# Where a scan's input copies stand among attention steps, in a hybrid block on one core

## The chip, the cores and the metric

The kernel runs on one core of a Trainium2 chip. The time is what the device takes for one execution, in microseconds (us); the median of several runs is given. Besides these runs one execution was taken by the profiler, and all rows below come from it.

The core has five engines that matter here, each with its own queue of instructions, done strictly in order: TensorE (PE in the rows; its weight loads are PEld), VectorE (DVE), ScalarE (ACT), GpSimd (POOL) and SyncE (SP), which issues the loads. An instruction waits on semaphores for what it needs from other engines, and all that stands behind it in its queue waits too.

## The reference, cut to what matters

One layer of a decoder on 512 positions of width 1024, in float32: a normalisation, an input projection, three token mixers on its parts, gates, an output projection and a residual, then a gated convolutional feed-forward part of inner width 2816 with its own normalisation and residual, and a last normalisation. Two of the three mixers are touched here:

```
proj = h @ w_in                                   # qa, ka, va, qd, kd, vd, u, g
ya   = banded_attention(qa, ka, va, 127, sinks)   # A: 8 heads, 4 blocks of 128 positions
x_t  = Abar * x_(t-1) + Bbar u_t                  # C: diagonal complex state space,
y    = Re(C x) + D u                              #    32 groups of 16 channels, 64 states each
out  = x + (gates * (ya, yb, yc) @ w_branch) @ w_out
```

B is a dilated attention that comes later in the kernel.

## The kernel before

Every large product is done in three TensorE passes: each operand is split into a high part and a low part of a rounded format (`whi`, `wlo` for weights), and high times high, high times low and low times high are summed in one PSUM bank (`mm3`, `mm3m`). ScalarE makes the high part of a weight (a copy, L66), VectorE the low one (a subtraction, L92); for some weights GpSimd does every second low part.

The work is a list of **units**, mostly one output tile of 128 x 512 each: 24 matmuls of 128 x 512. Unit 0 finishes the projection of `u`; units 1 to 4 are the queries of mixer A, 5 and 6 its keys and values (`kA`, `vA`), 7 to 14 its gates, 15 to 24 the projections of mixer B, 25 to 68 branch products, more gates and the gated unit of mixer C, 69 to 76 the output projection (`out_unit`), and then come the feed-forward units. Two units share one chunk of weights, loaded by SyncE into one of two `raw` buffers and split in two pieces.

The order within each engine's queue is the order in which the program emits the instructions. `run` walks the units. At unit `u` it emits first the splits that are due for the next chunk, then the steps that `before(u, ...)` has listed for this unit, and then the unit's matmuls and what uses their result:

```
fs = plan.get(u, []) + later
...
if u in AUX_FIRST:          # (7, 11, 15, 19, 33, 35)
    for f in fs: f()
    fs = []
...                          # splits of the next chunk, those listed in early
for f in fs: f()
fn()
```

In the units named in `AUX_FIRST` the listed steps come ahead of the splits. `early` lists (chunk, pieces) that are split in a given unit; a piece can only be split when one of four piece buffers is free, and a chunk that is due in the next unit is split in this one in any case. A chunk whose pieces are all split has the load of a later one issued.

The steps that are interleaved with units 3 to 24:

- `attn_a(i)`, one for each block of 128 queries, gives control back after each step. Step 1: score matmuls of four heads into two PSUM banks `sc` (L802), and masks with row maxima on VectorE (L809), which free these banks. Step 2: the same for the other four heads, then the exponentials on ScalarE (L818) and the scaling on VectorE (L308). Step 3: transposes (L832) and their copies. Step 4: products with the values (L838); for blocks 1 to 3 a second round of these, and `ya` at the end.
- `ssm_bd(j)`, `ssm_inj(j)`, `ssm_ob(j)`, `ssm_e(j)` prepare slice `j` of four of mixer C. `ssm_bd` ends with the four copies (VectorE, L663) that lay `u` out by position within groups of four as `US[j]`. `ssm_inj` transposes the input matrices into two `pt` banks and copies them out as `INJ[j]` (ScalarE), and fills `TZ[j]`. `ssm_cpow` computes the powers `Vw` on GpSimd, with temporaries `vt`. `ssm_e` computes tables `E` on GpSimd.
- `ssm_m1(j)`: first step, 16 small matmuls of `INJ[j]` with `US[j]` into two `sc` banks (L723), four products with `E`, and two scans on VectorE; second step, four products on VectorE and two on GpSimd that give the states `X`. `ssm_m2(j)`: 48 small matmuls of `US[j]` with `TZ[j]` and of `X` with `OB[j]`, copied out as `yS`.
- `to_nat` transposes the values of mixer A into a `pt` bank, unit 8.

Nearly all temporaries (`US`, `INJ`, `E`, `vt`, score tiles, `th`, and the results of projections) come from one pool `s` of 46 buffers. A request takes a buffer when the program emits it, and its first writer waits until the last user of the buffer's former content is done.

In `out_unit` the first call has SyncE load `x` again for the residual; the last matmul of a token tile is followed by the residual add on VectorE and a sum of squares on ScalarE. `ko[0]` to `ko[3]` are the four chunks of `w_out`, used in units 69 to 72 in this order, the last two again in 73 and 74.

Of the kernel before, what the change touches and what calls it, by code (L numbers as in the profile page):

```python
# [31 lines left out]
def hybrid_block(  # L32
# [19 lines left out]
    def slot(shape, dt=F32, name="s"):  # L52
        return sl.tile(shape, dt, tag="s", name=name)
# [4 lines left out]
    def bank(tag, shape=(128, 512), name=None):  # L58
        return psp.tile(list(shape), F32, tag=tag, bufs=PSB[tag], name=name or tag)
# [4 lines left out]
    def copy_act(o, i, scale=None):  # L64
        if scale is None:
            S.activation(o, i, AF.Copy)  # L66
        else:
            S.activation(o, i, AF.Copy, scale=scale)
# [165 lines left out]
    def before(u, *fns):  # L234
        plan.setdefault(u, []).extend(fns)
# [81 lines left out]
    def tt(o, a, b, op, eng=None):  # L317
        emit(lambda: (eng or V).tensor_tensor(o, a, b, op=op))  # L318
        return o
# [332 lines left out]
    def expand(dst, src, j, scale=None):  # L652

        for g in range(2):
            p = slice(64 * g, 64 * g + 64)
            copy_act(dst[p, :, :, g, :], src[p].rearrange("p k (t j) h -> p t k j h", j=4)[:, :, :, j, :], scale=scale)

    def ssm_bd(j):
        for i in range(2):
            expand(BDs[j % 2][i], W[0][:, i], j)  # L660
        US[j] = slot([128, 4, 128], name="us")
        for tau in range(4):
            V.tensor_copy(US[j][32 * tau:32 * tau + 32],  # L663
                          uT[0][32 * j:32 * j + 32].rearrange("p t (c a) -> p t c a", a=4)[:, :, :, tau])

    def ssm_inj(j):
        bd = BDs[j % 2]
        INJ[j] = [slot([128, 4, 128], name="inj") for _ in range(2)]
        for i in range(2):
            pb = bank("pt")  # L670
            for t in range(4):
                PE.transpose(pb[:, t * 128:(t + 1) * 128],
                             bd[i][:, t].rearrange("p k g h -> p (k g h)"), ident)
            copy_act(INJ[j][i][:, :, :], pb[:, :].rearrange("p (t c) -> p t c", t=4))
        pk = bank("o", (128, 4, 32))
        for t in range(4):
            for i in range(2):
                PE.matmul(pk[:, t, :], bd[i][:, t].rearrange("p k g h -> p (k g h)"),
                          V0b[i][:, 4 * t + j].rearrange("p g h -> p (g h)"), start=(i == 0), stop=(i == 1))
        tz = TZ[j]  # L680
        for ti in range(4):
            for to in range(ti + 1, 4):
                b = 3 - (to - ti)
                copy_act(tz[32 * ti:32 * ti + 32, :, to, :], pk[32 * b:32 * b + 32, :, :])
        for ti in range(4):
            tt(tz[32 * ti:32 * ti + 32, :, ti, :], pk[96:128, :, :],
               DI[0][96:128].rearrange("p (t j) c -> p t j c", j=4)[:, :, j, :], ADD)

    def ssm_ob(j):
        for i in range(2):  # L690
            expand(OB[j][i], Vw[0][:, i], j, None if i == 0 else -1.0)
# [5 lines left out]
    def ssm_e(j):  # L697
        def v(tab):
            return tab.rearrange("p (t j) b -> p t j b", j=4)[:, :, j, :]

        b = [v(t)[:, :, None, :].to_broadcast([128, 4, 8, 16]) for t in eb]
        a = [v(t)[:, :, :, None].to_broadcast([128, 4, 8, 16]) for t in ea]
        E = [slot([128, 4, 8, 16], name="E") for _ in range(2)]
        t0 = slot([128, 4, 8, 16], name="et")
        tt(E[0], b[0], a[0], MUL, G)
        tt(t0, b[1], a[1], MUL, G)
        tt(E[0], E[0], t0, SUB, G)
        tt(E[1], b[0], a[1], MUL, G)
        tt(t0, b[1], a[0], MUL, G)
        tt(E[1], E[1], t0, ADD, G)  # L710
        Es[j] = [e[:, :, :, :].rearrange("p t a b -> p (t a b)") for e in E]
        A4s[j] = slot([128, 4, 128], name="a4")
        V.tensor_copy(A4s[j], mag4.rearrange("p (t j) -> p t j", j=4)[:, :, j:j + 1].to_broadcast([128, 4, 128]))
        V.memset(A4s[j][:, :, 0:1], 0.0)

    def ssm_m1(j):
        Er, Ei = Es.pop(j)
        s = []
        inj = INJ.pop(j)
        for i in range(2):  # L720
            pb = bank("sc", (128, 4, 128))
            for t in range(4):
                PE.matmul(pb[:, t, :], inj[i][:, t, :], US[j][:, t, :], start=True, stop=True)  # L723
            s.append(pb[:, :, :].rearrange("p t c -> p (t c)"))
        a, b, zr, zi = (slot([128, 512], name="z")[:, :] for _ in range(4))
        tt(zr, s[0], Er, MUL)
        tt(a, s[1], Ei, MUL)
        tt(zi, s[1], Er, MUL)
        tt(b, s[0], Ei, MUL)
        tt(zr, zr, a, ADD, G)  # L730
        tt(zi, zi, b, SUB, G)
        a4 = A4s.pop(j)[:, :, :].rearrange("p t c -> p (t c)")
        V.tensor_tensor_scan(a, a4, zr, 0.0, op0=MUL, op1=ADD)
        V.tensor_tensor_scan(b, a4, zi, 0.0, op0=MUL, op1=ADD)
        yield
        X = [slot([128, 4, 128], name="X") for _ in range(2)]
        x3 = slot([128, 512], name="xt")[:, :]

        def sh(v):
            return v.rearrange("p (t c) -> p t c", c=128)[:, :, 0:127]  # L740

        for i in range(2):
            G.memset(X[i][:, :, 0:1], 0.0)
        tt(zr, a, Er, MUL)
        tt(x3, b, Ei, MUL)
        tt(X[0][:, :, 1:128], sh(zr), sh(x3), SUB, G)
        tt(zi, a, Ei, MUL)
        tt(b, b, Er, MUL)
        tt(X[1][:, :, 1:128], sh(zi), sh(b), ADD, G)
        Xs[j] = X  # L750
        yield

    def ssm_m2(j):
        if not yS:
            yS.append(y8([128, 4, T], name="yS"))
        X, tz, us, ob = Xs.pop(j), TZ.pop(j), US.pop(j), OB.pop(j)
        py = bank("o", (128, 4, 128))
        for t in range(4):
            PE.matmul(py[:, t, :], tz[:, t].rearrange("p a b -> p (a b)"), us[:, t, :], start=True, stop=False)
            for i in range(2):  # L760
                PE.matmul(py[:, t, :], ob[i][:, t].rearrange("p k g h -> p (k g h)"), X[i][:, t, :],
                          start=False, stop=(i == 1))
        for tau in range(4):
            o = yS[0][32 * j:32 * j + 32].rearrange("p t (c a) -> p t c a", a=4)[:, :, :, tau]
            copy_act(o, py[32 * tau:32 * tau + 32])


    def to_nat(src, name, strided=False):

        pb = bank("pt")  # L770
        v = src[:, :].rearrange("p (i r) -> p r i", r=4) if strided else src[:, :].rearrange("p (b i) -> p b i", b=4)
        for b in range(4):
            PE.transpose(pb[:, b * 128:(b + 1) * 128], v[:, b, :], ident)
        o = slot([128, 4, 128], name=name)
        copy_act(o, pb[:, :].rearrange("p (b c) -> p b c", b=4))
        return o

    proj = {}
# [10 lines left out]
    VA = []  # L789
# [677 lines left out]
        for ci in range(2):  # L1467
            add(ko[2 * half + ci], out_unit(ko[2 * half + ci], pair, half, ci, last))
    for u, i, n in ((63, 0, 1), (64, 0, 2), (65, 0, 3), (66, 0, 4), (66, 1, 1), (67, 1, 2), (68, 1, 3), (69, 1, 4),
                    (69, 2, 1), (70, 2, 2), (71, 3, 1), (72, 3, 2)):  # L1470
        early.setdefault(u, []).append((ko[i], n))
    u_up = len(units)
    for c in range(NF // 2):
# [52 lines left out]
    def st_(g):  # L1526
        return lambda: next(g)

    CP = ssm_cpow()
    A = [attn_a(i) for i in range(4)]  # L1530
    B = [attn_b(i) for i in range(2)]
    M = [ssm_m1(j) for j in range(4)]
    before(0, lambda: pump(99), ssm_b, lambda: pump(6), ssm_phase)
    before(1, lambda: pump(9))
    before(2, lambda: pump(9))
    before(3, lambda: ssm_bd(0))
    before(4, lambda: ssm_inj(0), lambda: ssm_bd(1), lambda: ssm_e(0), st_(CP))
    before(5, lambda: ssm_inj(1), lambda: ssm_bd(2))
    before(6, lambda: ssm_inj(2), lambda: ssm_bd(3), st_(CP), st_(A[0]))
    before(7, st_(A[0]), lambda: ssm_inj(3))  # L1540
    before(8, lambda: VA.append(to_nat(proj["vA"], "VA")), lambda: ssm_ob(0), lambda: ssm_ob(1))
    before(9, st_(A[0]), st_(M[0]), lambda: ssm_ob(2))
    before(10, lambda: ssm_ob(3), st_(A[0]), st_(M[0]), st_(A[1]))
    before(11, st_(A[1]))
    before(12, lambda: ssm_m2(0), lambda: ssm_e(1))
    before(13, st_(A[1]), st_(M[1]))
    before(14, st_(A[1]), st_(M[1]), st_(A[2]))
    before(15, st_(A[1]), st_(A[2]))
    before(16, lambda: ssm_m2(1), lambda: ssm_e(2))
    before(17, st_(A[2]), st_(M[2]))  # L1550
    before(18, st_(A[2]), st_(M[2]), st_(A[3]))
    before(19, st_(A[2]), st_(A[3]))
    before(20, lambda: ssm_m2(2), lambda: VB.setdefault(0, [to_nat(proj["vB", 0], "VB0")]), lambda: ssm_e(3))
    before(21, st_(A[3]), st_(M[3]), lambda: VB[0].append(to_nat(proj["vB", 0], "VB1", True)))
# [51 lines left out]
```

## Time and profile before

| | |
|---|---|
| median of 3 runs | 820.75 us (820.46 to 821.0) |
| the profiled execution | 820.41 us, of which 818.6 us are its span |
| TensorE busy | 796.6 us, 97% of the span |
| VectorE busy | 540.5 us, 66% |
| ScalarE busy | 392.8 us, 48% |
| GpSimd busy | 165.3 us, 20% |
| TensorE's granted clock, mean | 0.994 of full speed |

The span is the time from the first to the last instruction of the core; 1.8 us of the execution lie outside it. Busy times are sums over instructions. The matmuls are pipelined and their ends are modelled, so a TensorE that is busy throughout may still issue at a lower rate; the starts of its instructions tell more than its busy time.

### The profile page before, as it was taken

Reading aid. Unit: us, or ns where it says so; the run is one execution under the profiler, and the core shown is the slowest. Engines: PE = TensorE matmul, PEld = TensorE weight load, DVE = VectorE, ACT = ScalarE, POOL = GpSimd, SP = SyncE. Lnnn points to the kernel's source line nnn. Section 1 sums busy time; section 2 is a strip of 40 time slices with the busy share of each in tenths; the row PEclk is TensorE's granted clock in tenths of the full one; section 3 lists DMA queues with packets and bytes.
Section 4 is the critical chain, followed back from the end, with each engine's and each line's share of the span. In section 5 each row is a group of like instructions: output and inputs, shape, how many; then the busy total and the mean of one; then the engine's idle time right before and its main releaser. Section 6 shows DMA issues by size and latency. Waiting matters only on the chain.

```text
span 818.6 us, 10655 instructions
## 1 busy us (share of the span) xinstructions
PE 796.6 (97%) x4007; PEld 660.5 (81%) x4007; DVE 540.5 (66%) x1021; ACT 392.8 (48%) x725; POOL 165.3 (20%) x222
## 2 busy tenths in 40 slices
PE   8999799999999999999999999999999999999995
PEld 7978678788787888788887998888888888888884
DVE  7998676674636637363665456667666666888976
ACT  6446456456354555351434334444444444455553
POOL 6189723513200100014440000000000000011201
PEclk9999999999999999999999999999999999999998
DMA  8332031121322113122243253222333334589952
GB/s 245 104 104 82 21 103 53 52 73 53 81 95 66 54 52 104 63 92 102 104 187 121 64 186 111 99 79 83 101 103 102 104 104 128 207 241 347 294 157 102
DMA packets 76871, 94.70 MB, mean 116 GB/s; under 512 B 8944, under 2 KB 56340, under 8 KB 76820
## 3 DMA queue, kind: packets, MB, share of 16 engines
q1 hardware_dynamic: 73828, 88.74, 32.8%
q0 software_dynamic: 2992, 5.29, 3.8%
q8 instruction: 31, 0.51, 0.3%
q14 instruction: 20, 0.16, 0.1%
HBM read 89.80 MB, written 4.22 MB: 115 GB/s over the span
## 4 chain that ended last, share of the span: by engine, by line
PE 80%; POOL 8%; DVE 6%; ACT 2%; issue 2%; DMA 1%; POOLq 0%; SPq 0%; DVEq 0%; ACTq 0%
PE up L208 10%; PE up L209 10%; PE up L210 10%; PE mm L208 9%; PE mm L210 9%; PE mm L209 9%; PE p L214 4%; PE p L216 4%; PE p L215 4%; POOL esc L318 1%; POOL vt L318 1%; POOL t L318 1%; PE acc L215 1%; PE acc L216 1%; PE acc L214 1%
## 5 line engine op out<-in xcount | busy, mean ns | idle before, releaser
L92 DVE TENSOR_TENSOR wlo<-raw,whi 128x1024 fp32r<-128x1024 f32 (+1 forms) x104 | 123.0, 1192 | 94.5 <-ACT whi L66 94.4
L208 PE MATMUL up<-hTh,whi 128*128 128x512 f32 (+1 forms) x384 | 142.9, 372 | 0.0
L210 PE MATMUL up<-hTh,wlo 128*128 128x512 f32 (+1 forms) x384 | 142.8, 372 | 0.0
L209 PE MATMUL up<-hTl,whi 128*128 128x512 f32 (+1 forms) x384 | 142.8, 372 | 0.0
L66 ACT ACTIVATE whi<-raw 128x1024 fp32r<-128x1024 f32 (+1 forms) x126 | 126.1, 1013 | 18.3 <-PE p L216 10.6
L208 PE MATMUL mm<-hTh,whi 128*128 128x512 f32 (+1 forms) x336 | 133.1, 396 | 0.0
L210 PE MATMUL mm<-hTh,wlo 128*128 128x512 f32 (+1 forms) x336 | 130.1, 387 | 0.0
L209 PE MATMUL mm<-hTl,whi 128*128 128x512 f32 (+1 forms) x336 | 130.0, 387 | 0.0
L314 DVE SCALAR_TENSOR_TENSOR cc<-up,cpar,cc 128x511 f32<-128x511 f32 x88 | 65.9, 749 | 70.0 <-ACT cc L1146 68.4
L210 PEld LDWEIGHTS up<-hTh,wlo 128*128 128x128 f32 x384 | 72.4, 188 | 12.5
L208 PEld LDWEIGHTS up<-hTh,whi 128*128 128x128 f32 x384 | 72.4, 188 | 12.5
L209 PEld LDWEIGHTS up<-hTl,whi 128*128 128x128 f32 x384 | 72.4, 189 | 12.3
L208 PEld LDWEIGHTS mm<-hTh,whi 128*128 128x128 f32 x336 | 63.6, 189 | 14.5 <-issue 2.5
L1146 ACT ACTIVATE cc<-up,cpar 128x512 f32<-128x512 f32 x44 | 34.1, 775 | 85.2 <-PE up L210 85.2
L210 PEld LDWEIGHTS mm<-hTh,wlo 128*128 128x128 f32 x336 | 63.5, 189 | 13.0
L209 PEld LDWEIGHTS mm<-hTl,whi 128*128 128x128 f32 x336 | 63.7, 190 | 11.7
L185 POOL DMA_DIRECT2D raw<-in_w_down_dram x5 | 5.7, 1147 | 271.3 <-DVE wlo L92 221.1
L214 PE MATMUL p<-whi,op 128*128 128x512 f32 x146 | 56.9, 389 | 0.0
L216 PE MATMUL p<-whi,op 128*128 128x512 f32 x146 | 56.9, 389 | 0.0
L215 PE MATMUL p<-wlo,op 128*128 128x512 f32 x146 | 56.9, 389 | 0.0
L1028 ACT ACTIVATE th<-mm 128x512 f32<-128x512 f32 x24 | 14.3, 595 | 65.5 <-PE mm L210 65.4
L318 POOL TENSOR_TENSOR th<-th 128x512 f32<-128x512 f32 x15 | 23.8, 1607 | 69.9 <-DVE th L314 69.9
(314 smaller groups left out, 1386.9 us busy)
## 6 DMA issues: line engine op xcount, KB each, us to landing
raw<-in_w_up_dram SPq DMA_DIRECT2D x22, 1024.0 KB, 5.1
raw<-in_w_in_dram SPq DMA_DIRECT2D x18, 1024.0 KB, 5.1
raw<-in_w_down_dram SPq DMA_DIRECT2D x19, 512.0 KB, 8.1
big<-in_w_down_dram SPq DMA_DIRECT2D x16, 512.0 KB, 6.5
x<-in_x_dram SPq DMA_DIRECT2D x8, 512.0 KB, 6.9
raw<-in_w_in_dram SPq DMA_DIRECT2D x8, 512.0 KB, 5.2
raw<-in_w_out_dram SPq DMA_DIRECT2D x4, 1024.0 KB, 5.1
big<-in_w_down_dram POOLq DMA_DIRECT2D x5, 512.0 KB, 9.0
```

Source lines behind the costliest of these rows:

```text
L66: S.activation(o, i, AF.Copy)
L92: (lo_eng or V).tensor_tensor(view(lo), r, view(hi).bitcast(F32), op=ALU.subtract)
L208: PE.matmul(ps, wh, xh, start=first, stop=False)
L209: PE.matmul(ps, wh, xl, start=False, stop=False)
L210: PE.matmul(ps, wl, xh, start=False, stop=last)
L214: PE.matmul(ps, xh, wh, start=first, stop=False)
L215: PE.matmul(ps, xh, wl, start=False, stop=False)
L216: PE.matmul(ps, xl, wh, start=False, stop=last)
L314: emit(lambda: V.scalar_tensor_tensor(o, a, s, b, op0=op0, op1=op1))
L318: emit(lambda: (eng or V).tensor_tensor(o, a, b, op=op))
L1028: S.activation(t, ps, AF.Tanh, scale=0.5)
L1146: S.activation(dst, ps, AF.Identity, bias=cpar[:, 3, f:f + 1], scale=cpar[:, 2, f:f + 1])
```

## The change

The copies into `US[j]` become a function of their own, `ssm_us(j)`, and are called in units 7, 8, 10 and 11 and not in units 3 to 6, behind the attention step of their unit. In units 10, 14 and 18 the first step of the next attention block and the second step of the scan change places. The last chunk of output weights, `ko[3]`, is split in unit 70; it was listed for 71 and 72, of which 71 did both pieces.

```diff
     def ssm_bd(j):
         for i in range(2):
             expand(BDs[j % 2][i], W[0][:, i], j)
+
+    def ssm_us(j):
         US[j] = slot([128, 4, 128], name="us")
         for tau in range(4):
             V.tensor_copy(US[j][32 * tau:32 * tau + 32],
...
     for u, i, n in ((63, 0, 1), (64, 0, 2), (65, 0, 3), (66, 0, 4), (66, 1, 1), (67, 1, 2), (68, 1, 3), (69, 1, 4),
-                    (69, 2, 1), (70, 2, 2), (71, 3, 1), (72, 3, 2)):
+                    (69, 2, 1), (70, 2, 2), (70, 3, 2)):
         early.setdefault(u, []).append((ko[i], n))
...
-    before(7, st_(A[0]), lambda: ssm_inj(3))
-    before(8, lambda: VA.append(to_nat(proj["vA"], "VA")), lambda: ssm_ob(0), lambda: ssm_ob(1))
+    before(7, st_(A[0]), lambda: ssm_inj(3), lambda: ssm_us(0))
+    before(8, lambda: VA.append(to_nat(proj["vA"], "VA")), lambda: ssm_ob(0), lambda: ssm_ob(1), lambda: ssm_us(1))
     before(9, st_(A[0]), st_(M[0]), lambda: ssm_ob(2))
-    before(10, lambda: ssm_ob(3), st_(A[0]), st_(M[0]), st_(A[1]))
-    before(11, st_(A[1]))
+    before(10, lambda: ssm_ob(3), st_(A[0]), st_(A[1]), st_(M[0]), lambda: ssm_us(2))
+    before(11, st_(A[1]), lambda: ssm_us(3))
     before(12, lambda: ssm_m2(0), lambda: ssm_e(1))
     before(13, st_(A[1]), st_(M[1]))
-    before(14, st_(A[1]), st_(M[1]), st_(A[2]))
+    before(14, st_(A[1]), st_(A[2]), st_(M[1]))
     before(15, st_(A[1]), st_(A[2]))
     before(16, lambda: ssm_m2(1), lambda: ssm_e(2))
     before(17, st_(A[2]), st_(M[2]))
-    before(18, st_(A[2]), st_(M[2]), st_(A[3]))
+    before(18, st_(A[2]), st_(A[3]), st_(M[2]))
     before(19, st_(A[2]), st_(A[3]))
```

## Rows read from the trace of the kernel before

**Rows 1.** The page, busy time, share of the span and instructions of each engine.
```profile
PE 796.6 (97%) x4007; PEld 660.5 (81%) x4007; DVE 540.5 (66%) x1021; ACT 392.8 (48%) x725; POOL 165.3 (20%) x222
```

**Rows 2.** Waits of TensorE: who for whom, us in total, times, longest.
```profile
PE sc L802 <- DVE mxA L809: 3.1, 2, 2.0
PE pt L773 <- ACT inj L66: 3.0, 1, 3.0
...
PE acc L215 <- DVE wlo L92: 0.8, 1, 0.8
```

**Rows 3.** Stretches: length, then busy us of each engine, TensorE's clock, DMA.
```profile
86.00:109.00 23.00, 20.04 (x108) 16.96 (x108) 12.03 (x27) 15.27 (x42) 11.32 (x19) 0.93 0.14 46
98.30:101.70 3.40, 3.40 (x10) 2.62 (x9) 1.95 (x5) 3.31 (x8) 0.00 (x0) 0.51 0.00 0
138.00:430.00 292.00, 291.75 (x1495) 234.98 (x1494) 164.01 (x370) 135.44 (x285) 64.70 (x57) 1.00 0.27 86
```

**Rows 4.** Timeline of TensorE: start, us, instruction, [idle before and what ended it].
```profile
76.52 0.72 PE L802 MATMUL sc<-pj 64*128 64x128 f32 x8
...
82.32 0.39 PE L209 MATMUL mm<-hTl,whi 128*128 128x512 f32 x1
82.55 0.39 PE L210 MATMUL mm<-hTh,wlo 128*128 128x512 f32 x1
84.95 1.13 PE L802 MATMUL sc<-pj 64*128 64x128 f32 x8 [2.02 <-DVE mxA L809]
...
97.33 0.66 PE L773 MATMUL pt<-ident,pj 128*128 128x128 f32 x4 [2.96 <-ACT inj L66]
...
105.79 1.95 PE L723 MATMUL sc<-us,inj 128*128 128x128 f32 x16
...
122.12 1.81 PE L802 MATMUL sc<-pj 64*128 64x256 f32 x8 [1.14 <-DVE mxA L809]
...
140.15 0.48 PE L208 MATMUL mm<-hTh,whi 128*128 128x512 f32 x1
...
432.64 0.51 PE L215 MATMUL acc<-wlo,mh 128*128 128x512 f32 x1 [0.75 <-DVE wlo L92]
```

**Rows 5.** The chain that ended last, in order of time: start, us, what.
```profile
155.62 1.06 PE sc L802 x8
```

**Rows 6.** Timeline of VectorE, units 5 and 6.
```profile
70.25 1.22 DVE L318 TENSOR_TENSOR tz<-o,DI 32x128 f32<-32x128 f32 x4 [1.42 <-ACT tz L66]
71.48 5.22 DVE L663 COPY us<-uT 32x512 f32<-32x512 f32 x4
...
79.97 4.41 DVE L663 COPY us<-uT 32x512 f32<-32x512 f32 x4
```

**Rows 7.** The line of the copies: ns least, median, most; first and last start.
```profile
L663 DVE COPY us<-uT x16: 623/797/1624, 57.6 to 83.4; 32x512 f32<-32x512 f32 x16
```

**Rows 8.** Timelines of ScalarE and of GpSimd, end of unit 7.
```profile
96.68 1.28 ACT L66 ACTIVATE inj<-pt 128x512 f32<-128x512 f32 x2 [5.37 <-POOL Vw L318]
...
95.92 1.40 POOL L318 TENSOR_TENSOR Vw<-vt 128x256 f32<-128x256 f32 x2
```

**Rows 9.** Timeline of VectorE, units 7 to 12.
```profile
91.98 4.75 DVE L308 TENSOR_SCALAR smA<-smA,lA 128x128 f32<-128x128 f32 x8
...
117.19 0.69 DVE L318 TENSOR_TENSOR ya<-o,ya 128x512 fp32r<-128x512 f32 x1 [0.85 <-ACT ya L66]
...
121.30 0.41 DVE L809 CUSTOM_DVE_ANT_0 smA<-sc,maskA 128x256 f32<-128x256 f32 x1
...
125.06 1.08 DVE L314 SCALAR_TENSOR_TENSOR nmA<-mxA,nsink 128x8 f32<-128x8 f32 x1
...
133.91 1.22 DVE L92 TENSOR_TENSOR wlo<-raw,whi 128x1024 fp32r<-128x1024 f32 x1
```

**Rows 10.** Timelines of ScalarE and of VectorE, units 71 and 72.
```profile
430.28 1.99 ACT L66 ACTIVATE whi<-raw 128x1024 fp32r<-128x1024 f32 x2
...
427.64 0.69 DVE L318 TENSOR_TENSOR x<-x,acc 128x512 f32<-128x512 f32 x1 [4.19 <-DMA x<-in_x_dram]
```

## The prediction

> **What bounds the kernel now.** I began with the page. TensorE counts as busy for 796.6 us of a span of 818.6 us [rows 1], so no change of order among the other engines can win more than the waits of TensorE, plus what its clock loses behind them. The list of waits on TensorE alone is the second view: three of its entries lie at places that the diff touches, 3.1 us behind the mask of the attention scores, 3.0 us behind a copy of `inj`, 0.8 us behind the split of an output weight [rows 2]. The table of stretches is the third: from 138 to 430 us TensorE idles 0.25 us in 292, at full clock [rows 3], so whatever is won earlier is carried to the end and little is won there. In the same table the granted clock is 0.51 from 98.3 to 101.7 us, right behind the longest wait.
>
> TensorE's timeline gives the price of each wait. Matmuls of 0.39 us are issued 0.23 us apart (82.32, 82.55), so a wait shown as idle time costs 0.16 us more than the row says [rows 4].
>
> **The copies `US`, and the wait at 85 us.** `US[3]` stands at the end of unit 6 on VectorE, 79.97 to 84.38 us [rows 6], ahead of the masks of block 0's first scores. TensorE needs the banks that these masks free: it idles 2.02 us until 84.95, and the eight score matmuls then take 1.13 us where the eight of unit 6 took 0.72 [rows 4]. Without the copy the masks run from about 80.0, done well before 82.8. Gain 2.02 + 0.16 + (1.13 - 0.72) = 2.59 us.
>
> **The wait at 97 us.** The transposes of `vA` wait 2.96 us [rows 4] for the two copies of `inj` of slice 3, and ScalarE does these at 96.68 because it waited 5.37 us for GpSimd's last step of `Vw` (95.92) [rows 8]. The reference has no such dependence; it is a buffer's. The pool `s` hands out its 46 buffers and then always the one free longest. Counting requests in program order, `inj` of slice 3 is the 56th and 57th, and the eleven buffers free by then are, oldest first, `craw` (2), `braw` (2), `esc`, `wt` (2), `et`, `V0`, `vt` (2): it gets the two `vt`, which GpSimd writes until the end of `Vw`. With the four `US` requested behind it, it is the 52nd and 53rd and gets the two `wt`, whose last use is far back. The copies then follow block 0's exponentials at once, before TensorE is through unit 7. Gain 2.96 + 0.16 = 3.12 us. The clock: 0.51 over 3.40 us [rows 3] is 3.40 x 0.49 = 1.67 us, lost right behind an idle stretch of 3 us and, I take it, gone with it.
>
> The pair `vt` goes to `VA` and `US[1]` instead. On ScalarE `VA` then may wait for `Vw`, but behind it stand the copies into `OB`, which need `Vw` anyway, and the product with `VA` comes a whole unit later: nothing.
>
> **Where `US[0]` and `US[1]` go.** They land in units 7 and 8, where VectorE is busy for only 12.03 of 23 us [rows 3]; that idle time covers them. The tight point is `US[0]`: block 0's scaling ends at 91.98 + 4.75 = 96.73 [rows 9], 2.59 us earlier after the change, 94.1; 1.2 us of `TZ` adds follow [rows 6], then four copies at 0.62 us, the least of the sixteen, to 97.8, or 4.41 us in all, to 99.7 [rows 6, 7]. TensorE's scan matmuls of slice 0 need them at 105.79 - 7.4 = 98.4 [rows 4]. Upper bound 1.4 us, lower bound none; I take none, since without the copies in units 3 to 6 GpSimd's tables are through sooner and these copies then run beside an idle GpSimd.
>
> **Units 10 to 13.** Now the masks of block 1's first scores go ahead of the scan's second half. Before, TensorE waited 1.14 us at 122.12 for them, and the scores took 1.81 us where later ones take 1.06 [rows 4, 5]: gain 1.14 + 0.16 + 0.75 = 2.05 us. But VectorE must now do `US[2]` ahead of the second masks, and `US[3]` ahead of the low split of unit 13's weights (unit 11 is in `AUX_FIRST`). On the clock of before: `ya` ends at 117.88; first masks four times 0.41, 119.5; the scan's second half, 121.30 - 117.88 = 3.42, 122.9; `US[2]`; second masks 1.6; from there to the low split the chain takes 133.91 - 125.06 = 8.85 [rows 9]; `US[3]`; the split 1.2. For `US[2]` the bounds are 2.5 us (four of the fastest) and 5.22 us (from 71.48, beside GpSimd's tables `E` of slice 0; those of slice 1 now run beside it) [rows 6, 7]; I take 4.8, the mean of the two slow groups, since the tables are there. For `US[3]` 2.5, GpSimd being idle by then. The split ends at 122.9 + 4.8 + 1.6 + 8.85 + 2.5 + 1.2 = 141.9. TensorE needs it for the third matmul of unit 13, 140.15 + 0.46 [rows 4], less the 2.05 won: 138.6. So 3.3 us are lost there, part of it already at the transposes of block 1, which wait for its scaling. Unit 10 to 13 together: 1.25 us worse. The swaps in units 14 and 18 are costed at nothing: TensorE doesn't wait there now [rows 3], and the scan's result is needed two units later.
>
> **The output weights.** `ko[3]` is split now behind the squares of the first residual, at 430.28 on ScalarE, since both wait for `x` [rows 10]; TensorE loses 0.75 + 0.16 = 0.91 us at 432.64 [rows 4]. In unit 70 the split stands ahead of them. Its weights are loaded ahead of `x` on SyncE's queue, so they are there at 427.64 at the latest [rows 10]; two high splits of 1.0 and the first low one of 1.2 put it near 430, ahead of 431.6. What is queued behind, the residual add, comes some 2 us later; its bank is needed again four units on. The load of the next up weights is issued earlier, which nobody waits for. Gain 0.91, bounds 0 and 0.91.
>
> **Sum.** 2.59 + 3.12 + 1.67 + 2.05 - 3.3 + 0.91 = 7.04 us. The profiled execution took 820.41 us, 0.34 below the median shown; against the median, 820.75 - 7.04 = **813.7 us**.
>
> **The rivals.**
> A. `US[2]` costs little: 2.5 us instead of 4.8, so 1.0 us is lost in unit 13 and not 3.3; time 811.4, or 810.4 if no wait forms at all. For it: the median of the sixteen copies is 0.80 us [rows 7]. Against: the eight from 71 us on, beside GpSimd's large tables, took 9.6 us together [rows 6].
> B. Each copy beside GpSimd waits a whole GpSimd instruction: at 1.62 us, the slowest of the sixteen [rows 7], `US[2]` takes 6.5 us; time 815.4, and if the idle time in unit 13 drops the clock as it did at 98 us, 1.67 more, 817.1. Against it: the groups took 4.4 and 5.2, not 6.5. The Trainium skill, SBUF — State Buffer, "Who interferes with whom", says that a VectorE copy in a two-port mode and a GpSimd instruction exclude each other for a whole instruction; by that rule the time would be rival B's, and the trace agrees as far as copies of one shape took from 0.62 to 1.62 us.
> C. The buffer order is not as I count it and `inj` still waits for `Vw`: the 3.12 and 1.67 stay lost; time 820.75 - 2.25 = 818.5.
> D. Slower. VectorE falls so far behind in units 9 to 13 that the new wait exceeds all gains, 10.34 us. The price is 1 us for each us that unit 13's low split comes later than 138.6. `US[2]` and `US[3]` both at 6.5 us and `US[0]` late by 1.4 give 3.3 + 1.7 + 4.0 + 1.4 = 10.4, with a clock drop 12.1: 822.5. Against it: GpSimd has no tables left when `US[3]` runs.
>
> **How the numbers follow.** Forecast 0.58 (812 to 815.4), A 0.17, B 0.16, C 0.04, D 0.03, and 0.02 for no change. The worst sum of bounds short of D is `US[2]` 5.2, `US[3]` 4.4, `US[0]` late by 1.4: 7.0 us lost, 817.4. The range is 810.4 (A at its best) to 817.4; it leaves out C, D and a little of B. A difference under 0.2%, 1.6 us, can't be told from no change here. Faster 0.94, the same 0.03, slower 0.03.
>
> **What would show it.** Right: no wait of TensorE at 85 and 97 us, clock 1.00 throughout 80 to 110, `inj` of slice 3 copied right behind block 0's exponentials, no wait for a low split near 430. The new wait: some 3 us of TensorE idle about two units after the first masks of block 1, released by block 1's scaling and by a low split, with `US` copies of over 1 us shortly before. Wrong: a wait at the scan matmuls of slice 0 (US[0] late), no wait at all in unit 13 (A), or `inj` still released by GpSimd (C).

## The result

The changed kernel takes **815.75 us** (median of 4, 814.88 to 816.42), the kernel before, timed beside it, 820.73 us (820.46 to 821.0): ratio 0.9939, 95% interval 0.9925 to 0.9952. The forecast was 813.7, range 810.4 to 817.4. The profiled execution took 814.88 us, span 813.1.

The page of the kernel after, its row of busy times, and its list of waits of TensorE (who for whom, us in total, times, longest):

```profile
PE 795.6 (98%) x4007; PEld 658.8 (81%) x4007; DVE 538.8 (66%) x1021; ACT 392.8 (48%) x725; POOL 160.5 (20%) x222
```

```profile
PE mm L210 <- DVE wlo L92: 1.2, 1, 1.2
...
PE pt L834 <- DVE smA L308: 0.6, 1, 0.6
...
PE pt L775 <- ACT pj L66: 0.3, 1, 0.3
```

The three waits of [rows 2] are gone, and three shorter ones stand in their place. (Lines below the moved copies are two higher: L804 is the L802 of before.)

The stretches of the kernel after, columns as in [rows 3]:

```profile
80.00:103.00 23.00, 23.00 (x134) 19.57 (x133) 16.15 (x40) 16.93 (x46) 10.83 (x18) 1.00 0.18 59
126.00:131.00 5.00, 4.41 (x21) 2.81 (x20) 2.89 (x11) 4.36 (x12) 0.00 (x0) 1.00 0.00 2
131.00:145.00 14.00, 12.72 (x65) 8.97 (x64) 10.40 (x14) 9.37 (x12) 2.58 (x4) 1.00 0.23 75
```

TensorE is busy throughout from 80 to 103 us, at full clock, and idles 1.9 us between 126 and 145.

Its timeline after, the instructions that answer to [rows 4]:

```profile
82.57 0.71 PE L804 MATMUL sc<-pj 64*128 64x128 f32 x8
...
91.43 0.60 PE L775 MATMUL pt<-ident,pj 128*128 128x128 f32 x4
...
113.34 1.13 PE L804 MATMUL sc<-pj 64*128 64x256 f32 x8
...
128.86 2.17 PE L834 MATMUL pt<-ident,smA 128*128 128x128 f32 x8 [0.59 <-DVE smA L308]
...
134.49 0.50 PE L210 MATMUL mm<-hTh,wlo 128*128 128x512 f32 x1 [1.21 <-DVE wlo L92]
...
142.41 1.64 PE L804 MATMUL sc<-pj 64*128 64x256 f32 x8
...
193.27 0.66 PE L775 MATMUL pt<-ident,pj 128*128 128x128 f32 x4 [0.35 <-ACT pj L66]
```

Both programs issue the same 4007 matmuls and transposes in the same order, so the start of each can be taken from the start of its twin in the kernel before. That gives a running gain, 84.95 - 82.57 = 2.38 us at the scores of block 0, for instance, and its steps stand against the terms of the forecast. Each row of the table is taken at the first matmuls behind the place, when the new rate is reached. The first 0.30 us stand there already at 13 us, ahead of anything that the change moves; they belong to this pair of executions:

| place | start before | start after | running gain | step | forecast |
|---|---|---|---|---|---|
| end of unit 6 | 82.55 | 82.25 | 0.30 | +0.30 | 0 |
| behind the wait at 85 | 86.02 | 83.22 | 2.80 | +2.50 | +2.59 |
| behind the wait at 97 | 97.49 | 91.54 | 5.95 | +3.15 | +3.12 |
| clock, to 102 | 102.62 | 95.09 | 7.53 | +1.58 | +1.67 |
| scores of block 1 | 123.56 | 114.10 | 9.46 | +1.93 | +2.05 |
| unit 13 | 140.93 | 134.82 | 6.11 | -3.35 | -3.3 |
| unit 14 | 148.57 | 143.66 | 4.91 | **-1.20** | 0 |
| unit 20 | 198.00 | 193.65 | 4.35 | **-0.56** | 0 |
| output weights | 433.45 | 427.92 | 5.53 | +1.18 | +0.91 |

At the end of the trace it is 5.54 us, where the forecast's sum was 7.04.

The two steps that the forecast has at nothing come to 1.76 us. VectorE and ScalarE of the kernel after show where the first comes from:

```profile
94.07 2.48 DVE L665 COPY us<-uT 32x512 f32<-32x512 f32 x4
...
115.58 5.03 DVE L665 COPY us<-uT 32x512 f32<-32x512 f32 x4
...
128.45 2.19 DVE L308 TENSOR_SCALAR smA<-smA,lA 128x256 f32<-128x256 f32 x8
130.68 2.50 DVE L665 COPY us<-uT 32x512 f32<-32x512 f32 x4
133.21 2.36 DVE L92 TENSOR_TENSOR wlo<-raw,whi 128x1024 fp32r<-128x1024 f32 x2
```

```profile
88.42 1.06 ACT L66 ACTIVATE inj<-pt 128x512 f32<-128x512 f32 x2
...
133.27 4.37 ACT L66 ACTIVATE yS<-o 32x512 f32<-32x512 f32 x4 [2.92 <-DVE us L665]
137.66 0.60 ACT L1030 ACTIVATE th<-mm 128x512 f32<-128x512 f32 x1
138.16 1.05 ACT L66 ACTIVATE whi<-raw 128x1024 fp32r<-128x1024 f32 x1
139.10 1.08 ACT L66 ACTIVATE pTA<-pt 128x512 f32<-128x512 f32 x2
```

`US[0]` takes 0.62 us a copy, `US[2]` ahead of the second masks 1.26 in the mean, `US[3]` 0.62 again. ScalarE's copies into `yS` wait 2.92 us until `US[3]` is copied (130.68 + 2.50 = 133.18): `yS` takes over the large buffer of `uT`, whose last reader is now `US[3]` in unit 11, where it was in unit 6. `th`, a high split and `pTA` are queued behind.

### The profile page after: what moved, and what is told of

Same layout as the page of the kernel before. It is cut to its first block, busy times and chain, and to the rows that moved or that the text cites. A ratio compares the mean times of both kernels' runs of the same rounds, so it can differ in the third digit from the quotient of the medians.

```text
span 813.1 us, 10653 instructions
## 1 busy us (share of the span) xinstructions
PE 795.6 (98%) x4007; PEld 658.8 (81%) x4007; DVE 538.8 (66%) x1021; ACT 392.8 (48%) x725; POOL 160.5 (20%) x222
## 4 chain that ended last, share of the span: by engine, by line
PE 83%; DVE 11%; ACT 3%; issue 2%; POOL 1%; POOLq 0%; DVEq 0%
PE up L209 10%; PE up L210 10%; PE up L208 10%; PE mm L208 10%; PE mm L210 9%; PE mm L209 9%; PE p L214 4%; PE p L215 4%; PE p L216 4%; PE acc L215 2%; PE acc L214 2%; PE acc L216 2%; DVE us L665 2%; ACT smA L820 1%; DVE wlo L92 1%
```

## The experiments

Times are medians, each beside runs of the kernel before on the same chip. The executions of one kernel spread (the first below from 817.18 to 822.52 us), so differences of 1 us are read from the running gain, which a profile gives at each place. Here it is for all runs, in us, at the matmuls that start at the given time in the kernel before: behind unit 8, the scores of block 1, unit 13, unit 14, the scores of block 2, unit 20 and the output weights. Rows are best read by the steps within them: what two rows differ by in the first column can lie ahead of anything that their edits touch. In runs 6, 9 and 10 it does, since in their profiles the granted clock fell for some us near 60 us (to a mean of 0.61, 0.63 and 0.50 from 60 to 64 us), where it stayed at 1.00 in the kernels before and after. Each expectation sets a theory against a rival; "theory" below says that the result came out as the theory has it.

| run | 102.62 | 123.56 | 140.93 | 148.57 | 157.19 | 198.00 | 433.45 |
|---|---|---|---|---|---|---|---|
| after | 7.53 | 9.46 | 6.11 | 4.91 | 4.90 | 4.35 | 5.53 |
| 1 copies alone | 7.44 | 7.09 | 5.81 | 4.61 | 2.74 | 2.75 | 2.64 |
| 2 swaps alone | 0.21 | 2.11 | 2.11 | 2.11 | 2.11 | 1.54 | 1.41 |
| 3 output weights alone | -0.08 | -0.02 | -0.02 | -0.02 | -0.02 | -0.04 | 1.15 |
| 4 old buffers, late copies | 7.52 | 9.45 | 5.57 | 4.37 | 4.36 | 3.78 | 4.94 |
| 5 `inj` requested early | -4.85 | -4.82 | -4.83 | -4.83 | -4.83 | -4.85 | -4.95 |
| 6 new buffers, late `Vw` | 5.97 | 7.29 | 2.55 | 1.47 | 1.42 | 0.85 | 2.07 |
| 7 longer wait of `yS` | 7.33 | 9.26 | 5.75 | 2.21 | 2.21 | 1.64 | 2.88 |
| 8 `US[3]` on ScalarE | 7.22 | 9.15 | 7.23 | 7.20 | 7.20 | 6.64 | 7.86 |
| 9 `US[2]` on ScalarE | 5.90 | 7.83 | 7.83 | 6.80 | 6.77 | 6.20 | 7.39 |
| 10 both on ScalarE | 3.85 | 5.78 | 5.78 | 5.78 | 5.79 | 5.21 | 6.41 |
| 11 both, old order in unit 18 | 7.40 | 9.33 | 9.33 | 9.33 | 9.33 | 9.28 | 10.46 |
| 12 both in unit 11 | 2.38 | 4.29 | 3.26 | 1.77 | 1.77 | 1.20 | 2.40 |

**1. The copies alone.** The kernel after with the old order in units 10, 14 and 18, and the old split of `ko[3]`:

```diff
-    before(10, lambda: ssm_ob(3), st_(A[0]), st_(A[1]), st_(M[0]), lambda: ssm_us(2))
+    before(10, lambda: ssm_ob(3), st_(A[0]), st_(M[0]), st_(A[1]), lambda: ssm_us(2))
...
-    before(14, st_(A[1]), st_(A[2]), st_(M[1]))
+    before(14, st_(A[1]), st_(M[1]), st_(A[2]))
```

> The kernel after, but the scan's second step stands ahead of the next block's scores again in units 10, 14 and 18, and the last output weights are split in unit 71 again; only the copies of US stand late. Theory (behind unit 9 it is VectorE's queue up to the low split of unit 13 that sets the time, so the 1.74 us that the swap won at the scores of block 1 are given back in full within units 11 to 13): the change without the swap keeps the same end of units 10 to 14, loses only the 1.0 us of the output weights, and gains 0.5 us at 193 us if that small loss comes from the swap in unit 18; 816.3 to 816.8 us. Rival (the two add up: the swap is worth its own 1.7 us whatever stands behind): 818.4 us. Either way: no waits at 85 and 97 us, clock at 1.00 there.

Measured: 819.34 us (12 runs; before 820.49), the profiled one 817.94. The theory's 816.3 to 816.8 us is missed; the time is nearer to the rival's 818.4, but not for its reason. TensorE in this run:

```profile
134.78 0.50 PE L210 MATMUL mm<-hTh,wlo 128*128 128x512 f32 x1 [1.00 <-DVE wlo L92]
...
152.13 1.82 PE L804 MATMUL sc<-pj 64*128 64x256 f32 x8 [1.12 <-DVE mxA L811]
```

Behind unit 13 the running gain is 5.81 us, against 6.11 with the swap: up to there the swap of unit 10 is worth 0.30 us (0.1 of which the two profiles differ by from the start) and not the 1.93 that it wins at the scores, as the theory has it. But block 2's scores now wait for their masks in unit 14 and 4.61 - 2.74 = 1.87 us are lost. So with the copies made late the swap of unit 14 has a use that it has not in the kernel before: it holds off a wait that the copies would bring.

**2. The swaps alone**, on the kernel before (the same three lines the other way).

> The kernel before with the three swaps alone (scores ahead of the scan's second step in units 10, 14 and 18). Theory (without US copies in units 10 and 11 VectorE has the time that the swap needs): the wait at 122 us goes, 1.7 to 2.05 us are won there and not given back in unit 13; 0.5 us is lost near 197 us; 819.0 to 819.5 us. Rival (the scan's second step, late by some 3 us, costs as much elsewhere): 820.7 us, no change.

Measured: 819.01 us (before 820.49). The 1.90 us won at the scores of block 1 (0.21 to 2.11) are kept through units 13 and 14; 0.57 are lost in unit 20, behind a wait of 0.4 us for `pj`. As the theory has it.

**3. The output weights alone**, on the kernel before.

```diff
-                    (69, 2, 1), (70, 2, 2), (71, 3, 1), (72, 3, 2)):
+                    (69, 2, 1), (70, 2, 2), (70, 3, 2)):
```

> The kernel before with the last output weights split in unit 70 and nothing else. Theory: the wait for their low part at 433 us goes, 0.9 to 1.0 us; 819.8 us. Rival (their load is not there in time and the splits hold up what follows): 820.7 us or above.

Measured: 819.11 us (before 820.49); 1.19 us are won at the place (-0.04 to 1.15). Theory. This profile shows something else too: the granted clock fell behind the wait at 85 us, not behind that at 97:

```profile
86.30:97.00 10.70, 10.70 (x41) 9.37 (x41) 6.92 (x20) 3.59 (x18) 10.70 (x18) 0.56 0.00 0
97.00:103.00 6.00, 6.00 (x30) 4.97 (x29) 3.03 (x6) 5.77 (x13) 0.36 (x1) 1.00 0.00 0
```

TensorE fell 4.8 us behind its twin (91.03 before, 95.87 here) and was level again by 102 us: the wait at 97 us and the half clock behind it, which cost the kernel before 3.12 and 1.58 us, are not in this profile.

**4. The old buffers, late copies.** What made `inj` come sooner? The forecast put it down to the order in which the pool hands out buffers. Here `US` is requested where it was, so `inj` of slice 3 has the pair `vt` again.

```diff
     def ssm_bd(j):
...
+        US[j] = slot([128, 4, 128], name="us")
+        V.memset(US[j][:, :, 0:1], 0.0)
...
     def ssm_us(j):
-        US[j] = slot([128, 4, 128], name="us")
```

> The kernel after, with the buffers of US requested in units 3 to 6 as in the kernel before (a one-column memset on VectorE is their first writer), and the copies late as after. So inj of slice 3 gets the two buffers of vt again, as in the kernel before. Theory 1 (the wait at 97 us went because the order of the buffers changed): the copies of inj wait for GpSimd's last step of Vw again; as that step now ends near 90.8 us and not at 97.3, they would run at 91, and TensorE would wait 0.5 to 2 us at its transposes, without a drop of the clock; 816 to 818 us. Theory 2 (the wait went because GpSimd, no longer beside the copies, ends Vw 6.5 us sooner, and the buffers hardly matter): within 0.6 us of the kernel after, 815.2 to 816.4 us. If Vw is late again although the copies are gone: 819 to 820 us.

Measured: 815.46 us (before 820.49), as the kernel after; no wait at 91 us. ScalarE in this run:

```profile
90.33 1.30 ACT L66 ACTIVATE inj<-pt 128x512 f32<-128x512 f32 x2 [1.69 <-POOL Vw L318]
```

`inj` does wait for `Vw`, which shows that the buffers were counted rightly, but `Vw` ends 6.3 us sooner than before (91.0 us; before, 95.92 + 1.40 = 97.3 [rows 8]), because GpSimd no longer works beside sixteen copies, and that is soon enough.

**5. The buffers alone**, on the kernel before.

```diff
+    def inj_early(j):
+        INJ[j] = [slot([128, 4, 128], name="inj") for _ in range(2)]
+        for t in INJ[j]:
+            V.memset(t[:, :, 0:1], 0.0)
...
-    before(5, lambda: ssm_inj(1), lambda: ssm_bd(2))
+    before(5, lambda: ssm_inj(1), lambda: ssm_bd(2), lambda: inj_early(3))
```

> The kernel before, copies in their old places, with the two buffers of inj of slice 3 requested in unit 5 (a one-column memset on VectorE is their first writer) and not in unit 7, so that they are two whose last users are done long before, and not the pair vt. Theory (the order of the buffers alone takes the wait at 97 us away, as GpSimd's sooner end of Vw alone did with the old buffers): TensorE's wait of 2.96 us at 97 us goes, 3.1 us; the stretch of half clock behind it goes too unless it comes behind the wait at 85 us instead; 815.7 us, or 817.4 us with the stretch. Rival (Vw holds the copies by something other than the buffers): no change, 820.5 us.

Measured: 825.69 us (before 820.73; ratio 1.0059, 1.0047 to 1.0071). A miss of both, and slower. The pair `vt` went to the score tiles of block 0 instead, and VectorE's masks waited for GpSimd:

```profile
96.72 0.29 DVE L815 CUSTOM_DVE_ANT_0 smA<-sc,maskA 128x128 f32<-128x128 f32 x1 [11.32 <-POOL Vw L318]
```

So the pair is a real hazard for whoever gets it, but this run doesn't say whether order alone would have been enough.

**6. New buffers, late `Vw`.** The other half of the same question: the kernel after, with GpSimd held up by doing the tables of slice 0 twice.

```diff
-        tt(E[0], b[0], a[0], MUL, G)
...
+        for _ in range(2 if j == 0 else 1):
+            tt(E[0], b[0], a[0], MUL, G)
...
```

> The kernel after, with GpSimd doing its six table operations for slice 0 twice, some 7 us more, so that the last step of Vw ends near 97.5 us as in the kernel before, while the order of the buffers is that of the kernel after. Theory (the order of the buffers suffices as well): the copies of inj of slice 3 stay right behind block 0's exponentials at 88 us and TensorE's transposes at 91 us don't wait; VA, which has a buffer of vt, waits for Vw to 97.5 us and all of ScalarE's queue behind it, 2 to 4 us lost in units 8 and 9; 818 to 819 us. Rival (the sooner end of Vw was the only cause): inj waits again, TensorE idles some 6 us at 91 us; 820 us or above, with the clock's drop.

Measured: 818.25 us (before 820.59). ScalarE and GpSimd in this run:

```profile
90.33 1.06 ACT L66 ACTIVATE inj<-pt 128x512 f32<-128x512 f32 x2
...
96.98 0.60 ACT L66 ACTIVATE VA<-pt 128x512 f32<-128x512 f32 x1 [1.24 <-POOL Vw L318]
```

```profile
96.20 1.45 POOL L318 TENSOR_TENSOR Vw<-vt 128x256 f32<-128x256 f32 x2
```

`Vw` ends as late as before, and `inj` doesn't wait: the theory. Either the order of the buffers or the sooner `Vw` suffices, and the change does both. `VA` inherits the wait, 1.24 us here; the expectation of 2 to 4 us lost right there was too high (5.97 us at 102.62 fall to 5.40 at 114, by 0.57). Of the 5.53 - 2.07 = 3.46 us between this profile and that of the kernel after, 1.57 are the clock near 60 us, ahead of what the run changes; the larger part of the rest is the loss up to unit 13, 7.29 - 2.55 = 4.74 us against 3.35, where VectorE is later still. So the time is near the theory's, but in this profile partly by chance; that `inj` doesn't wait is read from the row and not from the time.

**7. A longer wait of `yS`.** This run was meant to take the wait of `yS` away by giving it another of the three large buffers.

```diff
         if not yS:
+            V.memset(y8([128, 4, T], name="skip")[:, :, 0:1], 0.0)
             yS.append(y8([128, 4, T], name="yS"))
```

> The kernel after, with one request more in the pool of three large buffers ahead of yS (a one-column memset on VectorE, behind US[3]), so that yS takes the buffer of W, last read in unit 6, and not that of uT, last read by US[3]. Theory (the 1.1 us lost in unit 14 are ScalarE's wait of 2.9 us for US[3] ahead of the copies into yS): that wait goes, th, the high splits and pTA of units 13 and 14 come 2.9 us sooner, TensorE regains 1.1 us; 814.6 us. Rival (they are lost to VectorE's lateness as such, the low split at 139 us): no gain, 815.6 us.

Measured: 818.87 us (before 820.73), the profiled one 817.55. The request did the reverse: `yS` now waits for the small memset, which stands behind a low split in VectorE's queue. ScalarE and TensorE in this run:

```profile
136.04 4.30 ACT L66 ACTIVATE yS<-o 32x512 f32<-32x512 f32 x4 [5.34 <-DVE skip L757]
```

```profile
142.44 1.56 PE L841 MATMUL o<-pTA,VA 128*64 128x512 f32 x4 [2.32 <-ACT pTA L66]
```

Both expectations, 814.6 and 815.6 us, are missed. That is a dose instead of a cure. The wait of `yS` grew by 5.34 - 2.92 = 2.42 us, and the loss in unit 14 from 1.20 to 5.75 - 2.21 = 3.54 us, by 2.34: there TensorE pays for each further microsecond of ScalarE's wait.

**8 and 9. `US[3]` or `US[2]` on ScalarE.** Each of the two late groups of copies by itself leaves VectorE:

```diff
-    before(10, lambda: ssm_ob(3), st_(A[0]), st_(A[1]), st_(M[0]), lambda: ssm_us(2))
-    before(11, st_(A[1]), lambda: ssm_us(3))
+    before(10, lambda: ssm_ob(3), st_(A[0]), st_(A[1]), st_(M[0]), lambda: ssm_us(2), lambda: ssm_us(3, copy_act))
+    before(11, st_(A[1]))
```

> The kernel after, with the copies of US[3] alone on ScalarE, at the end of unit 10's list; US[2] stays on VectorE ahead of the second masks. Theory (the two copies cost by their places: US[2] delays block 1's scaling, US[3] delays the low split of unit 13 and, by the buffer that yS takes over, ScalarE in unit 14): the waits for the low split and of yS go, the wait for the scaling at 129 us stays; of the 3.0 + 1.1 us lost there some 1.5 to 1.8 stay; 813.2 us. Rival (it is US[2] alone, at 5.0 us, that makes VectorE late): no gain, 815.6 us.

Measured: 812.80 us (before 820.59; ratio 0.9901, 0.9888 to 0.9914). Theory: of the 4.55 us lost in units 13 and 14 (9.46 - 4.91), 9.15 - 7.20 = 1.95 stay, all at one wait of TensorE and the slow transposes behind it:

```profile
129.21 2.17 PE L835 MATMUL pt<-ident,smA 128*128 128x128 f32 x8 [0.63 <-DVE smA L308]
```

For the other group, in unit 9:

```diff
-    before(9, st_(A[0]), st_(M[0]), lambda: ssm_ob(2))
-    before(10, lambda: ssm_ob(3), st_(A[0]), st_(A[1]), st_(M[0]), lambda: ssm_us(2))
+    before(9, st_(A[0]), st_(M[0]), lambda: ssm_ob(2), lambda: ssm_us(2, copy_act))
+    before(10, lambda: ssm_ob(3), st_(A[0]), st_(A[1]), st_(M[0]))
```

> The kernel after, with the copies of US[2] alone on ScalarE, at the end of unit 9's list; US[3] stays on VectorE in unit 11. Theory (the 5.0 us of US[2] beside GpSimd's tables are what VectorE has too little room for; the 2.5 us of US[3] fit): no wait for the scaling nor for the low split in unit 13, US[3] is done by 128 us, so no loss by yS either; 811.5 us. Rival (US[3] ahead of the low split costs its 2.5 us whatever comes before): 813 to 814 us.

Measured: 811.31 us (before 820.59; ratio 0.9897, 0.9874 to 0.9920); nothing is lost in unit 13, and 7.83 - 6.80 = 1.03 us in unit 14. Theory for the first, but not for the second: `yS` still waits 3.32 us for `US[3]`. ScalarE in this run:

```profile
131.34 4.40 ACT L66 ACTIVATE yS<-o 32x512 f32<-32x512 f32 x4 [3.32 <-DVE us L666]
```

So the loss in unit 14 goes with this wait, and not with VectorE's low split, for which TensorE doesn't wait in unit 13 here. The two groups are not a sum: without `US[3]` on VectorE 2.60 us come back, without `US[2]` 3.52, of 4.55.

**10 and 11. Both on ScalarE, with and without the swap of unit 18.** First the two edits above together (`US[2]` in unit 9, `US[3]` in unit 10):

> The kernel after, with the copies of US[2] and US[3] on ScalarE, at the end of the lists of units 9 and 10, and not on VectorE in units 10 and 11. Theory (the loss of units 13 and 14 is the 7.5 us of these copies in VectorE's queue and the yS wait behind them): the waits for block 1's scaling and for the low split in unit 13 and the wait of yS go; 3.0 + 1.1 us less; 811.5 us. Rival (ScalarE's copies hold up th, the high splits or the exponentials as much): 815 us or above.

Measured: **810.53 us** (before 820.73; ratio 0.9886, 0.9870 to 0.9902). Theory: nothing is lost in units 13 and 14 (5.78 throughout; the profiled execution was the longest of five, 814.0 us, with 3.4 us lost to the clock near 60 us). A group takes 4.53 us on ScalarE, which is idle there:

```profile
105.66 4.53 ACT L66 ACTIVATE us<-uT 32x512 f32<-32x512 f32 x4
```

Then also without the swap of unit 18:

```diff
-    before(18, st_(A[2]), st_(A[3]), st_(M[2]))
+    before(18, st_(A[2]), st_(M[2]), st_(A[3]))
```

> As the kernel with the copies of US[2] and US[3] on ScalarE, and in unit 18 the scan's second step again ahead of the scores of block 3. Theory (the 0.5 us lost at 193 us come from that swap: the scan's GpSimd products then run beside VectorE's small steps ahead of block 3's exponentials): no wait of the transposes for pj in unit 20; 0.5 us less, 811.0 us. Rival (without the swap the scores of block 3 wait for their banks, as those of block 2 did without theirs): 1.5 us more, 813 us.

Measured: 810.96 us (before 820.73; ratio 0.988, 0.9867 to 0.9893). The scores of block 3 don't wait without the swap, and the wait for `pj` in unit 20 is gone; the medians of the two kernels can't be told apart. But all fourteen profiles agree on the place: in the nine with the swap of unit 18, the small addition ahead of block 3's exponentials takes 0.98 us and 0.55 to 0.58 us are lost in unit 20; in the five without it, 0.17 us, and at most 0.05 lost. It delays ScalarE's exponentials, and behind these stands the copy `pj`. The kernel after, and this run:

```profile
186.63 0.98 DVE L318 TENSOR_TENSOR esA<-sink,nmA 128x8 f32<-128x8 f32 x1
```

```profile
182.51 0.17 DVE L318 TENSOR_TENSOR esA<-sink,nmA 128x8 f32<-128x8 f32 x1
```

**12. One place later on VectorE.** `US[2]` moves behind the second masks and the scaling:

```diff
-    before(10, lambda: ssm_ob(3), st_(A[0]), st_(A[1]), st_(M[0]), lambda: ssm_us(2))
-    before(11, st_(A[1]), lambda: ssm_us(3))
+    before(10, lambda: ssm_ob(3), st_(A[0]), st_(A[1]), st_(M[0]))
+    before(11, st_(A[1]), lambda: ssm_us(2), lambda: ssm_us(3))
```

> The kernel after, with the copies of US[2] one place later in VectorE's queue: in unit 11, behind block 1's second masks and scaling, right ahead of those of US[3]. Theory (place and company set their cost, not their number: behind the scaling VectorE has waited 4.2 us for the exponentials, and GpSimd's tables are done): the four take 2.5 us and not 5.0; no wait for the scaling; the low split of unit 13 at about 132 us, at most 0.5 us lost; 811.5 to 812 us. Rival (the same copies in the same units cost the same): 815.6 us.

Measured: 814.75 us (before 820.59; ratio 0.9934, 0.9913 to 0.9955), six runs from 813.17 to 818.19. The copies cost what the theory says, eight in 5.00 us where `US[2]` alone took 5.03, and no transposes wait for the scaling; but `US[3]` ends at 136.02 us, so `yS` can't start sooner (it starts at 136.39, by the profile behind a scan matmul of TensorE), and 4.29 - 1.77 = 2.52 us are lost in units 13 and 14. The theory's 811.5 to 812 us is missed, the rival's reason is out, and the best runs are between the two times. The profiled execution was the longest of the six, 818.19 us, by something that comes ahead of all that the edit moves; VectorE in this run:

```profile
84.25 6.63 DVE L314 SCALAR_TENSOR_TENSOR nmA<-mxA,nsink 128x8 f32<-128x8 f32 x1
90.92 0.17 DVE L318 TENSOR_TENSOR esA<-sink,nmA 128x8 f32<-128x8 f32 x1
...
131.02 5.00 DVE L665 COPY us<-uT 32x512 f32<-32x512 f32 x8
```

and GpSimd beside it, then TensorE and its clock:

```profile
85.71 1.44 POOL L318 TENSOR_TENSOR Vw<-vt 128x256 f32<-128x256 f32 x2
87.10 2.38 POOL L318 TENSOR_TENSOR vt<-Vw,t 128x256 f32<-128x256 f32 x4
89.42 1.45 POOL L318 TENSOR_TENSOR Vw<-vt 128x256 f32<-128x256 f32 x2
```

```profile
94.94 1.11 PE L775 MATMUL pt<-ident,pj 128*128 128x128 f32 x4 [3.39 <-ACT inj L66]
```

```profile
95.00:98.00 3.00, 3.00 (x10) 2.52 (x11) 2.41 (x11) 2.89 (x8) 0.00 (x0) 0.50 0.00 0
```

A step of 128x8 elements that takes 0.32 us in the profile of the kernel after ended only when GpSimd's last step did (89.42 + 1.45 = 90.87). `inj` comes at 94.31 us and not at 88.42, and the wait at 97 us of the kernel before is back, with half the clock behind it.

## Why the prediction was right, and where it was off

The measured 815.75 us lies in the range, 810.4 to 817.4, but outside the forecast's own band, 812 to 815.4: it falls into the band of rival B, whose mechanism did not happen (`US[2]` took 5.03 us and not 6.5). The range had that room for dearer copies; two other losses filled it, which is luck. The mechanism of each term was as forecast, but for the cause of one and for two losses that no term has:

- **The wait at 85 us** (2.59): right, 2.50.
- **The wait at 97 us** (3.12): the size is right, 3.15; the cause is half of it. The forecast named the order of the buffers alone. Runs 4 and 6 show that the order suffices and that the sooner end of `Vw`, which the forecast mentions only for `US[0]`, suffices too. Rival C is run 4, and cost nothing.
- **The clock** (1.67): 1.58 in this pair of profiles. Run 3 shows that the place of the drop varies from one execution to the next; the term is right only for an execution in which it fell behind this wait.
- **`US[0]` and `US[1]`** at nothing: right, no wait at the scan matmuls of slice 0.
- **Scores of block 1** (2.05): 1.93.
- **Unit 13** (-3.3): -3.35, in the two parts forecast, the transposes of block 1 and the low split, with `US[2]` at 5.03 us (forecast 4.8) and `US[3]` at 2.50 (2.5). Runs 8 and 9 put the whole loss down to these eight copies; rivals A and B, which have `US[2]` at 2.5 and 6.5, are out.
- **The step that failed** is one that was missing, costed at nothing: the sum followed the copies' own queue and the tiles that they write, and not the tile that they *read*. Moving the last reader of `uT` from unit 6 to unit 11 holds its buffer, `yS` gets it, and ScalarE waits 2.92 us: -1.20 us in unit 14. Run 7 shows the cause by its dose; runs 8 and 10 show the loss gone where `US[3]` ends early.
- **"The swaps in units 14 and 18 are costed at nothing"**: that of unit 18 costs 0.56 us (runs 2 and 11). That of unit 14 is worth 1.87 us once the copies are late (run 1), so it had to be there for the forecast's zero.
- **The output weights** (0.91, bounds 0 and 0.91): 1.19 alone, 1.18 in the whole, above the upper bound. The forecast counts 0.16 us beside the idle time of a wait; here some 0.4 stand beside it, as the matmuls on both sides take 0.51 us and not 0.39 [rows 4], and the one behind 432.64 starts 0.34 us later and not 0.23.

The two missing losses, 1.20 + 0.56 = 1.76 us, are more than the 1.50 us by which the traced gain of 5.54 falls short of 7.04. The forecast's six terms came to 6.99 us together, and the other 0.30 is what the two executions differ by from the start. Of the 2.05 us between 813.7 and 815.75 the rest is in the spread of the runs.

The forecast cited the Trainium skill, SBUF — State Buffer, "Who interferes with whom", for a copy that is shut out for one whole GpSimd instruction. The four copies of `US[2]` took 0.60, 1.61, 1.38 and 1.40 us, against 0.61 to 0.64 for those of the other groups, beside GpSimd's operations of 1.43 us: no copy was held for much longer than one such operation, and their sum came out between forecast and rival B. One instruction doesn't cover the 6.63 us of run 12; there the measurement decides.

## What to carry to other kernels

Moving a step late moves the release of everything that it reads as well as the arrival of what it writes: look up who gets those buffers next and which queue then waits. A step that is taken off a busy queue by delay can come back as a loss where that queue is next needed: `US[0]` and `US[1]` came back at no cost in units 7 and 8, `US[2]` and `US[3]` cost 4.55 us in units 13 and 14. An engine that is idle at that place (ScalarE here, two groups of 4.5 us) turns 815.75 into 810.5 to 811.0 us with the same work. And when a change shifts both buffers and times, an effect may have two sufficient causes, which only runs that undo one at a time can show.

## What the runs showed of the hardware

- A VectorE step with two inputs in SBUF seems to be held off, at times, through many GpSimd instructions and not only one: 6.63 us for 128x8 elements, starting at 84.25 us and ending 0.01 us behind GpSimd's chain of eleven. In the profile of the kernel after the step of the same block that follows the exponentials took 2.31 us (88.55 to 90.86), to the end of the same chain, and was hidden. That GpSimd is what holds it is read from these ends; no run took GpSimd's work away. It differs by execution and by place: six profiles of kernels with the same order there gave 0.32 to 0.48 us for the first step, and in the kernel before the other step took 0.36 us (at 91.34) beside GpSimd steps of the same kind. It may explain part of the spread of the medians; that was not tested.
- TensorE's granted clock can fall to about half, the lower of its two levels (1.2 and 2.4 GHz), behind one wait in one execution and behind another in the next: behind 97 us [rows 3], behind 85 us (run 3), and in the profiles of runs 6, 9 and 10 behind waits of 0.8 and 0.2 us near 58 us, which the kernel after has too, at 1.00. What a drop cost here depended on whether a later wait took it up: 1.58 us at 98 us, some 3.3 us near 60 us in run 10, nothing measurable at 86.
- The same 32x512 copy costs 0.62 us on VectorE alone, up to 1.61 us on VectorE beside GpSimd, and 1.13 us on ScalarE (4.53 for four). GpSimd pays too: its products of 128x512 for the tables of slice 1 took 1.43 us beside the copies of `US[2]` and 1.05 behind them.
